# A hybrid GLA/SGU/PEER block on one core: other group sizes in the front, separate gather queues, and work moved between VectorE and GpSimd

## The chip, the core and the metric

The kernel runs on one core of a Trainium2 chip. The metric is the device time in microseconds (us) of one execution. A core has TensorE (PE; weight loads are listed as PEld), VectorE (DVE), ScalarE (ACT), GpSimd (POOL) and SyncE (SP), each with its own instruction stream, and 16 DMA engines that they share. SP starts most of the plain transfers; POOL starts the gathers, which fetch 128 rows by a list of indices.

## The reference, cut to what matters

```python
h = x + merged(GLA branch, SGU branch) @ w_out          # 1024 tokens, width 1024
n2 = rmsnorm(h, norm2_g)
# peer(n2):
q = (n2 @ w_q).reshape(T, 8, 2, 128)                    # 8 heads, two halves
s1, s2 = q[:, :, 0] @ sub_k1.T, q[:, :, 1] @ sub_k2.T   # 128 scores each
v1, i1 = top_k(s1, 16); v2, i2 = top_k(s2, 16)
cand = v1[..., :, None] + v2[..., None, :]              # 16 x 16 a head
vals, ci = top_k(cand, 16)
idx = i1[ci // 16] * 128 + i2[ci % 16]                  # 128 experts a token
gates = softmax(vals)
hid = einsum('tkd,td->tk', expert_u[idx], n2)           # 16384 experts in all
out = einsum('tk,tkd->td', gelu(hid) * gates, expert_v[idx])
y = rmsnorm(h + out, final_g)
```

All arrays are float32.

## The kernel before

The 1024 tokens are eight blocks of 128. The program has four stages.

**Front** (`front_all`): projections, both branches, the merge, the queries and their scores, for a group of blocks at a time. `GROUPS` gives the groups and, by a letter, each block's kind. Each group reads every weight block again: `load_w` loads 512 KB (`wraw`), ScalarE rounds it to a high half (`whi`, L242), GpSimd subtracts that from it (`wlo`, L243), and three matmuls per chunk (high by high, high by low, low by high) make one product of float32 quality (`mm3`; the tiles `pt` and `pn`).

**Top-k** (`topk_steps`, L583 to L654) runs on VectorE: per head the sixteen largest of both score halves, the sums of the candidates (`cd`, L605, four rectangles a head), the sixteen largest sums, then the decoding into expert numbers and gates. It is a queue of small steps, and so is the gathering; after each group of matmuls `pump(us)` gives every `Queue` a credit of `us` times its rate and runs steps for it. What of the queues is not done by the end is run by `drain()`.

**Blocks of kind g** fetch their experts. `u_steps`: 128 gathers of u rows (`gu`, POOL L741), and for each a dot with the block's row on VectorE (L735). `v_steps`: 128 gathers of v rows (`gv`, L822), four to a step, which 32-column matmuls (L809) sum into `gacc` in PSUM; after the last, VectorE adds `gacc` to the residual (`gres`, L834). The block that `ROWV` names is summed by rows instead: gather (L785), then a multiply-add on VectorE (`racc`, L781). In `all_v` the blocks go one after the other. A gather waits for a free buffer and, through `paced`, for the last matmul put out ahead of it.

**Blocks of kind d** compute all 16384 experts. `gate_steps` builds their gate matrix from one-hot rows: `gJ` on VectorE (L686), `gW` half on GpSimd (L692, with the gate already multiplied in) and half on ScalarE (a Square and a Relu, L695 and L696); products `gp` (L674) go to `g_d` in DRAM. `h_phase(i)` makes the hidden values of 128 experts for the four d blocks: 24 matmuls of 512 columns (`hp`, L914 to L916). `v_phase` multiplies four such sets of gated values with four blocks of v: 96 matmuls (`vp`, L973 to L975) into 8 PSUM tiles, each added to `dacc` on VectorE (L978). `split` rounds u and v blocks to halves: the high one on ScalarE (L900), the low one (`ul`, `vl`) on VectorE (L901). There are 128 `h_phase`s and 32 `v_phase`s. The first `HEAD` = 80 `h_phase`s run before the first `v_phase` and store their values (`a_d`); this is the *head*. The rest are mixed among the `v_phase`s, the *body*, by the list `order`. The *drain* is what follows the last `v_phase`.

```python
GROUPS = ("ggdd", "ggdd")
HEAD = 80
ROWV = (2,)
```

Tile buffers: three for `gu`, six for `gv`, two for `wraw`, three that u and v blocks share (`raw`), four each for `vh` and `vl`.

Of the kernel before, what the change touches and what calls it, by code (L numbers as in the profile page):

```python
# [33 lines left out]
GROUPS = ("ggdd", "ggdd")  # L34
HEAD = 80
# [4 lines left out]
GUB = 3  # L40
WZB = 2
ARB = 2
UAHEAD = 2
VAHEAD = 3
ROWV = (2,)
WRB = 2
TGB = 4
GAHEAD = 3
GPOOL = 2
RATE_TOPK = 0.55  # L50
RATE_TOPK2 = 1.0
RATE_UF = 0.75
RATE_UH = 1.0
RATE_GATHER = 0.9
# [12 lines left out]
def block_kernel(ctx: ExitStack, tc: tile.TileContext, a, out):  # L67
# [43 lines left out]
    S = {"state": state0}  # L111
# [115 lines left out]
    def front_all(groups, pump, after_group):  # L227
# [6 lines left out]
        def load_w(src, c0, n):  # L234
# [90 lines left out]
        def sgu_block(G, b):  # L325
# [23 lines left out]
        def decay_block(G, b):  # L349
# [5 lines left out]
            z = G["scr"][:, 4 + b, :]  # L355
# [52 lines left out]
        def branches(G):  # L408
# [20 lines left out]
            G["scr"] = fp.tile([P, 8, 512], F32, name="scr", tag="nBl")  # L429
# [135 lines left out]
        for n, G in enumerate(Gs):  # L565
            branches(G)
# [16 lines left out]
    def topk_steps(b, G):  # L583
# [7 lines left out]
        rc = tk.tile([P, HEADS], F32, name="rc")  # L591
        for h in range(HEADS):
# [5 lines left out]
            v = tk.tile([P, 2, TOPK], F32, name="v")  # L598
            for half in range(2):
                top16(v[:, half, :], ix[:, half, hs], s[:, half, :])  # L600
            cd = tk.tile([P, NCAND], F32, name="cd")
            o = 0
            for a0, na, nbb in RECTS:
                sh = [P, na, nbb]
                nc.vector.tensor_tensor(  # L605
                    cd[:, o:o + na * nbb].rearrange("p (i j) -> p i j", i=na),
                    v[:, 0, a0:a0 + na].unsqueeze(2).to_broadcast(sh),
                    v[:, 1, 0:nbb].unsqueeze(1).to_broadcast(sh), op=ALU.add)
                o += na * nbb
            yield 3.9  # L610
            top16(vals[:, hs], pos[:, hs], cd)
            yield 1.4
# [45 lines left out]
    def gate_steps(gb, b):  # L658
# [23 lines left out]
        for q in range(P // 4):  # L682
# [30 lines left out]
    ws, iTs, iis, wz, hvs = {}, {}, {}, [], {}  # L713

    def start_v(gv):
        pools["gatv"] = gv
        for r in range(WZB):
            wz.append(gv.tile([P, 4, 64], F32, name=f"wz{r}"))
            nc.vector.memset(wz[r], 0.0)
        pools["fg"] = bcast_row(gv, a["gf"], D, "fg")  # L720

    def gather_steps():
# [48 lines left out]
        def v_rows(b):  # L771
# [11 lines left out]
            for k in range(HK):  # L783
                v = pools["gatv"].tile([P, D], F32, name="gv", bufs=GVB)
# [8 lines left out]
            finish(gat, b, acc, pools["fg"], pools["gatv"].tile([P, D], F32, name="gv", bufs=GVB))  # L793
            yield 0

        def v_steps(b):
# [38 lines left out]
            finish(gat, b, res, pools["fg"], flat)  # L835
# [42 lines left out]
    def pump(us):  # L878
        for q in queues:
# [7 lines left out]
    def dense(pump):  # L887
        TP = TB // 2 if TB > 512 else TB
        NP = TB // TP
        with tc.tile_pool(name="dn", bufs=1) as dn, ExitStack() as dvx:  # L890
# [3 lines left out]
            def split(pool, dst, src):  # L894
# [50 lines left out]
            def gates(i):  # L945
                key, at = i < HEAD, i // G2
                if held.get(key, (None, None))[0] != at:
                    G = dv.tile([P, NB, P // GT, G2, GT], F32, name="G", bufs=4)
# [3 lines left out]
                    held[key] = at, G  # L952
                return held[key][1][:, :, :, i % G2, :]
# [27 lines left out]

            order, fresh = [], list(range(HEAD, P))
            for i in range(HEAD):
                k = (i + 1) * len(fresh) // HEAD - i * len(fresh) // HEAD
                order += [i] + fresh[len(order) - i:len(order) - i + k]
            prev, cur = None, []
            for n, i in enumerate(order):
# [10 lines left out]
                if len(cur) == GI or n == P - 1:  # L998
# [77 lines left out]
```

## Time and profile before

| | us |
|---|---|
| runs | 3521.14, 3527.49, 3520.89; median 3521.14 |
| the profiled execution | 3520.11 |
| its span (first to last instruction) | 3518.3 |
| PE busy | 3062.6 (87%) |
| DVE busy | 2272.3 (65%) |
| POOL busy | 1818.8 (52%) |
| ACT busy | 1028.0 (29%) |

| moment in the span | us |
|---|---|
| first dot with a gathered u row | 632.0 |
| first matmul of an `h_phase` | 1188.0 |
| first matmul of a `v_phase` | 1955.7 |
| last matmul of a `v_phase` | 3213.2 |

Busy times are sums of an engine's instructions over the whole span, so they hide what binds a stage; the moments above cut the span into the four stages. Matmuls are pipelined: their records overlap, and the distance between two starts, not the length of one, is what a matmul costs. The column PEclk of the windows view is the granted TensorE clock as a share of its full 2.4 GHz.

### The profile page before, as it was taken

Reading aid. Unit: us, or ns where it says so; the run is one execution under the profiler, and the core shown is the slowest. Engines: PE = TensorE matmul, PEld = TensorE weight load, DVE = VectorE, ACT = ScalarE, POOL = GpSimd, SP = SyncE. Lnnn points to the kernel's source line nnn. Section 1 sums busy time; section 2 is a strip of 40 time slices with the busy share of each in tenths; the row PEclk is TensorE's granted clock in tenths of the full one; section 3 lists DMA queues with packets and bytes.
Section 4 is the critical chain, followed back from the end, with each engine's and each line's share of the span. In section 5 each row is a group of like instructions: output and inputs, shape, how many; then the busy total and the mean of one; then the engine's idle time right before and its main releaser. Section 6 shows DMA issues by size and latency. Waiting matters only on the chain.

```text
span 3518.3 us, 41416 instructions
## 1 busy us (share of the span) xinstructions
PE 3062.6 (87%) x14244; PEld 2217.4 (63%) x14244; DVE 2272.3 (65%) x4978; ACT 1028.0 (29%) x1898; POOL 1818.8 (52%) x1433
## 2 busy tenths in 40 slices
PE   7999998878768589999999889999999798886665
PEld 6978987766656367666666666656667676674110
DVE  4262457999978768567533676555558999996000
ACT  3332333122122356526553222222222222221000
POOL 3334332556556588838784445444443566644443
PEclk9999998989879799999999999999999999997676
DMA  3223442566677878788779988899889999997776
GB/s 126 78 91 115 148 127 76 181 214 205 221 259 245 281 273 308 284 318 286 288 269 332 347 297 328 320 340 324 318 312 310 319 370 376 373 344 239 239 241 207
DMA packets 336548, 908.72 MB, mean 258 GB/s; under 512 B 33857, under 2 KB 124225, under 8 KB 335314
## 3 DMA queue, kind: packets, MB, share of 16 engines
q0 software_dynamic: 147456, 536.94, 43.5%
q1 hardware_dynamic: 188882, 369.14, 30.4%
q8 instruction: 112, 1.84, 0.2%
q14 instruction: 98, 0.80, 0.1%
HBM read 830.45 MB, written 75.50 MB: 257 GB/s over the span
## 4 chain that ended last, share of the span: by engine, by line
PE 46%; DVE 21%; DMA 14%; issue 11%; POOL 5%; ACT 1%; POOLq 0%; DVEq 0%; SPq 0%; ACTq 0%
PE gacc L809 8%; DMA gu<-in_pu,ii 7%; DVE gu L735 6%; DMA gv<-in_pv,iT 5%; PE hp L914 4%; PE hp L916 4%; PE hp L915 4%; POOL gu L741 3%; PE vp L973 3%; PE vp L974 3%; PE vp L975 3%; DVE racc L781 3%; PE gp L674 2%; PE pt L248 2%; PE pt L249 2%
## 5 line engine op out<-in xcount | busy, mean ns | idle before, releaser
L741 POOL DMA_INDIRECT gu<-in_pu,ii x512 | 595.9, 1164 | 565.5 <-DVE gu L735 324.2
L735 DVE SCALAR_TENSOR_TENSOR gu<-gu,gn 128x1024 f32<-128x1024 f32 x512 | 672.8, 1322 | 180.0 <-DMA gu<-in_pu,ii 167.6
L822 POOL DMA_INDIRECT gv<-in_pv,iT x384 | 414.8, 1080 | 553.7 <-PE gacc L809 463.9
L243 POOL TENSOR_TENSOR wlo<-wraw,whi 128x1024 fp32r<-128x1024 f32 x144 | 351.8, 2461 | 424.0 <-ACT whi L242 423.4
L809 PE MATMUL gacc<-gv,wz 128*32 128x512 f32 x1536 | 452.5, 724 | 108.3 <-DMA gv<-in_pv,iT 106.9
L914 PE MATMUL hp<-dnh,uh 128*128 128x512 f32 x1024 | 414.9, 405 | 54.1 <-ACT uh L900 52.8
L973 PE MATMUL vp<-vh,ah 128*128 128x512 f32 x1024 | 407.4, 407 | 42.2 <-DVE dacc L978 26.1
L974 PE MATMUL vp<-vl,ah 128*128 128x512 f32 x1024 | 413.4, 404 | 7.6 <-DVE vl L901 7.6
L916 PE MATMUL hp<-dnh,ul 128*128 128x512 f32 x1024 | 410.2, 401 | 7.5 <-DVE ul L901 7.0
L915 PE MATMUL hp<-dnl,uh 128*128 128x512 f32 x1024 | 409.7, 400 | 2.0 <-DVE dnl L178 2.0
L975 PE MATMUL vp<-vh,al 128*128 128x512 f32 x1024 | 396.0, 402 | 6.5 <-DVE al L962 6.5
L809 PEld LDWEIGHTS gacc<-gv,wz 128*32 128x32 f32 x1536 | 75.5, 119 | 357.9 <-DMA gv<-in_pv,iT 212.6
L692 POOL TENSOR_SCALAR gW<-iota_r,gT 128x128 f32<-128x128 bf16 x256 | 276.5, 1087 | 23.5 <-PE gp L674 11.8
L914 PEld LDWEIGHTS hp<-dnh,uh 128*128 128x128 f32 x1024 | 195.4, 191 | 129.7 <-ACT uh L900 65.5
L973 PEld LDWEIGHTS vp<-vh,ah 128*128 128x128 f32 x1024 | 199.3, 195 | 116.6 <-DVE dacc L978 43.7
L978 DVE TENSOR_TENSOR dacc<-dacc,vp 128x512 f32<-128x512 f32 x256 | 168.2, 683 | 122.7 <-PE vp L975 114.3
L974 PEld LDWEIGHTS vp<-vl,ah 128*128 128x128 f32 x1024 | 199.2, 195 | 67.4 <-issue 16.8
L916 PEld LDWEIGHTS hp<-dnh,ul 128*128 128x128 f32 x1024 | 194.4, 190 | 74.1 <-issue 21.8
L975 PEld LDWEIGHTS vp<-vh,al 128*128 128x128 f32 x1024 | 198.3, 194 | 67.6 <-issue 15.9
L901 DVE TENSOR_TENSOR ul<-raw,uh 128x1024 fp32r<-128x1024 f32 x128 | 157.3, 1229 | 125.0 <-ACT uh L900 96.5
L785 POOL DMA_INDIRECT gv<-in_pv,ii x128 | 178.7, 1396 | 114.3 <-DVE racc L781 45.6
L915 PEld LDWEIGHTS hp<-dnl,uh 128*128 128x128 f32 x1024 | 195.8, 191 | 56.6 <-issue 16.8
(271 smaller groups left out, 5737.6 us busy)
## 6 DMA issues: line engine op xcount, KB each, us to landing
raw<-in_ut SPq DMA_DIRECT2D x128, 512.0 KB
raw<-in_pv SPq DMA_DIRECT2D x128, 512.0 KB
wraw<-in_wt SPq DMA_DIRECT2D x80, 512.0 KB
g_d<-gst SPq DMA_DIRECT2D x8, 4096.0 KB
G<-g_d SPq DMA_DIRECT2D x256, 128.0 KB
a_d<-A SPq DMA_DIRECT2D x80, 256.0 KB
Ar<-a_d SPq DMA_DIRECT2D x80, 256.0 KB
wraw<-in_wq SPq DMA_DIRECT2D x32, 512.0 KB
```

Of the source, the lines that this page charges most:

```text
L243: nc.gpsimd.tensor_tensor(lo[:, :, sl], raw, hi[:, :, sl].bitcast(F32), op=ALU.subtract)
L692: nc.gpsimd.tensor_scalar(W[:, x, :], iota_r, i_, g_, op0=ALU.is_equal, op1=ALU.mult)
L735: queued(nc.vector.scalar_tensor_tensor(u, u, 1.0, n2, op0=ALU.mult, op1=ALU.mult, accum_out=hv[:, k:k + 1]), "dve")
L741: paced(nc.gpsimd.indirect_dma_start(out=u, out_offset=None, in_=a["pu"], in_offset=bass.IndirectOffsetOnAxis(ap=ii[:, k:k + 1], axis=0)))
L809: queued(nc.tensor.matmul(acc[32 * g:32 * g + 32, dh, :], z[:, g, 31 - r:63 - r], vs[g][:, dh * 512:(dh + 1) * 512], start=r == 0, stop=r ...
L822: paced(nc.gpsimd.indirect_dma_start(out=v, out_offset=None, in_=a["pv"], in_offset=bass.IndirectOffsetOnAxis(ap=iTs[b][:, t:t + 1], axis=0)))
L914: nc.tensor.matmul(ps[:, :TP], uh[:, cs], nh[:, c, ts_], start=c == 0, stop=False)
L915: nc.tensor.matmul(ps[:, :TP], uh[:, cs], nl[:, c, ts_], start=False, stop=False)
L916: mm = nc.tensor.matmul(ps[:, :TP], ul[:, cs], nh[:, c, ts_], start=False, stop=c == DC - 1)
L973: nc.tensor.matmul(ps, ah[:, bl], vh[:, ds_], start=x == 0, stop=False)
L974: nc.tensor.matmul(ps, ah[:, bl], vl[:, ds_], start=False, stop=False)
L975: mm = nc.tensor.matmul(ps, al[:, bl], vh[:, ds_], start=False, stop=x == n - 1)
```

## The change

- `GROUPS` becomes three groups of 2, 3 and 3 blocks. Blocks 0 to 3 are still of kind g and 4 to 7 of kind d. `HEAD` is 72. Each weight block is read three times instead of twice; in group 0 `wlo` is made on VectorE.
- The gathers' one queue, which took u and v steps in turns, becomes two with rates of their own; a u dot stands four gathers behind its gather instead of two; there are five `gu` buffers. The last g block (3) is the one summed by rows, not block 2.
- The candidate sums of all eight heads are made together: four operations a block instead of 32.
- `gW` is made on VectorE like `gJ`, for four tokens in one operation, and ScalarE multiplies the gates in. GpSimd and the Square/Relu pair have no part in it any more.
- `vl` is made on GpSimd instead of VectorE; u and v blocks have staging buffers of their own (three `rawu`, two `rawv`).
- The gate tiles `G` are held for one pair of indices; `order` sorts pairs of `h_phase`s; `fg` is loaded for each block that ends; some scratch tiles shrink with the group. `GVX` is 0, so its extra tiles are never taken.

```diff
-GROUPS = ("ggdd", "ggdd")
-HEAD = 80
+GROUPS = ("gg", "ggd", "ddd")
+HEAD = 72
-GUB = 3
+RAWB = {"u": 3, "v": 2}
+GUB = 5
-UAHEAD = 2
+UAHEAD = 4
-ROWV = (2,)
-WRB = 2
-TGB = 4
-GAHEAD = 3
+ROWV = (3,)
+WRB = 3
+TGB = 5
+GAHEAD = 2
-RATE_UF = 0.75
-RATE_UH = 1.0
-RATE_GATHER = 0.9
+RATE_U = (0.4, 0.9, 0.8)
+RATE_V = (0.2, 0.5, 0.5)
+RATE_VE = 1.2
...
-                nc.gpsimd.tensor_tensor(lo[:, :, sl], raw, hi[:, :, sl].bitcast(F32), op=ALU.subtract)
+                eng = nc.gpsimd if S["group"] else nc.vector
+                eng.tensor_tensor(lo[:, :, sl], raw, hi[:, :, sl].bitcast(F32), op=ALU.subtract)
...
+        o = 0
+        for a0, na, nbb in RECTS:
+            sh = [P, HEADS, na, nbb]
+            nc.vector.tensor_tensor(
+                cd[:, :, o:o + na * nbb].rearrange("p h (i j) -> p h i j", i=na),
+                v[:, :, 0, a0:a0 + na].unsqueeze(3).to_broadcast(sh),
+                v[:, :, 1, 0:nbb].unsqueeze(2).to_broadcast(sh), op=ALU.add)
+            o += na * nbb
...
+            queued(nc.vector.tensor_tensor(W, T[:, 0, qs].unsqueeze(2).to_broadcast([P, 4, P]),
+                                           iota_r.unsqueeze(1).to_broadcast([P, 4, P]), op=ALU.is_equal), "dve")
             for x in range(4):
                 t = 4 * q + x
-                i_, g_ = T[:, 0, t:t + 1], T[:, 2, t:t + 1]
-                if x < GPOOL:
-                    nc.gpsimd.tensor_scalar(W[:, x, :], iota_r, i_, g_, op0=ALU.is_equal, op1=ALU.mult)
-                else:
-
-                    queued(nc.scalar.activation(W[:, x, :], iota_r, AF.Square, scale=-1.0, bias=i_), "act")
-                    nc.scalar.activation(W[:, x, :], W[:, x, :], AF.Relu, scale=T[:, 3, t:t + 1], bias=g_)
+                queued(nc.scalar.activation(W[:, x, :], W[:, x, :], AF.Copy, scale=T[:, 2, t:t + 1]), "act")
...
     def pump(us):
+        if not q_u.its:
+            q_v.rate = RATE_VE
         for q in queues:
             q.run(us)
...
-                raw = dn.tile([P, D], F32, name="raw", bufs=3)
+                raw = pool.tile([P, D], F32, name="raw" + dst, bufs=RAWB[dst])
                 nc.sync.dma_start(raw, src)
                 nc.scalar.activation(hi, raw, AF.Copy)
-                last["dve"] = nc.vector.tensor_tensor(lo, raw, hi.bitcast(F32), op=ALU.subtract).ins
+                if dst == "u":
+                    last["dve"] = nc.vector.tensor_tensor(lo, raw, hi.bitcast(F32), op=ALU.subtract).ins
+                else:
+                    nc.gpsimd.tensor_tensor(lo, raw, hi.bitcast(F32), op=ALU.subtract)
...
+            pairs = sorted(range(P // G2), key=lambda n: (n + 0.5) / HEAD if n * G2 < HEAD
+                           else (n - HEAD // G2 + 0.5) / (P - HEAD))
+            order = [n * G2 + x for n in pairs for x in range(G2)]
...
-    q_topk, q_gat = Queue(RATE_TOPK), Queue(RATE_UF, turns=True)
+    q_topk, q_u, q_v = Queue(RATE_TOPK), Queue(RATE_U[0]), Queue(RATE_V[0])
...
-    q_gat.its.extend(gather_steps())
+    for q, it in zip((q_u, q_v), gather_steps()):
+        q.its.append(it)
```

What this does to the order of instructions is seen on GpSimd. In the front before, from its first weight block on:

```order
L243 TENSOR_TENSOR wlo<-wraw,whi 128x8x128 x88
L741 DMA gu<-in_pu,ii 128x1024 x4
L243 TENSOR_TENSOR wlo<-wraw,whi 128x8x128 x2
L741 DMA gu<-in_pu,ii 128x1024 x3
L243 TENSOR_TENSOR wlo<-wraw,whi 128x8x128
```

And after (L246 and L751 are the same two lines of code):

```order
L246 TENSOR_TENSOR wlo<-wraw,whi 128x8x128 x18
L751 DMA gu<-in_pu,ii 128x1024 x3
L246 TENSOR_TENSOR wlo<-wraw,whi 128x8x128 x2
L751 DMA gu<-in_pu,ii 128x1024 x2
L246 TENSOR_TENSOR wlo<-wraw,whi 128x8x128 x2
```

Of the 216 subtractions 76 are VectorE's (the 72 of group 0 and four of group 1 that are loaded during group 0's merge) and 140 GpSimd's, and the gathers begin after 18 instead of 88 of those that are left. In the body, GpSimd's row before had gathers alone:

```order
L741 DMA gu<-in_pu,ii 128x1024 x3
L822 DMA gv<-in_pv,iT 128x1024 x4
L741 DMA gu<-in_pu,ii 128x1024 x3
L822 DMA gv<-in_pv,iT 128x1024 x4
L741 DMA gu<-in_pu,ii 128x1024 x3
```

After, `vl` (L916) stands between them, two at a time, with nine gathers from pair to pair:

```order
L832 DMA gv<-in_pv,iT 128x1024 x4
L916 TENSOR_TENSOR vl<-rawv,vh 128x1024 x2
L751 DMA gu<-in_pu,ii 128x1024 x5
L832 DMA gv<-in_pv,iT 128x1024 x4
L916 TENSOR_TENSOR vl<-rawv,vh 128x1024 x2
L751 DMA gu<-in_pu,ii 128x1024 x5
```

GpSimd's end before, with the second half of block 3's four-row gathers (L822) after all others:

```order
L785 DMA gv<-in_pv,ii 128x1024
L741 DMA gu<-in_pu,ii 128x1024 x2
L822 DMA gv<-in_pv,iT 128x1024 x6
L741 DMA gu<-in_pu,ii 128x1024 x32
L822 DMA gv<-in_pv,iT 128x1024 x122
```

And after (L832 is the four-row gather, L795 the gather by rows):

```order
L916 TENSOR_TENSOR vl<-rawv,vh 128x1024 x2
L832 DMA gv<-in_pv,iT 128x1024 x4
L916 TENSOR_TENSOR vl<-rawv,vh 128x1024 x2
L832 DMA gv<-in_pv,iT 128x1024 x18
L795 DMA gv<-in_pv,ii 128x1024 x128
```

The last 128 gathers are now those of the block summed by rows, each of them followed by an add on VectorE, and 18 four-row gathers stand between the last `vl` and them. On TensorE 30 `gacc` matmuls follow the last `vp` where 256 did; 234 stand ahead of the first `vp` (256 before), and 504 among the `v_phase`s (256 before). The first `vp` comes after 74 `h_phase`s (81 before).

## Rows read from the trace of the kernel before

**Rows 1.** The page, its first part: busy time, share of the span, instructions.

```profile
PE 3062.6 (87%) x14244; PEld 2217.4 (63%) x14244; DVE 2272.3 (65%) x4978; ACT 1028.0 (29%) x1898; POOL 1818.8 (52%) x1433
```

**Rows 2.** Windows: stretch, length, busy us of PE, PEld, DVE, ACT, POOL; PEclk, DMA, GB/s.

```profile
0.00:470.00 470.00, 446.41 (x2648) 387.14 (x2649) 188.18 (x473) 166.21 (x296) 168.84 (x78) 0.99 0.35 112
470.00:1188.00 718.00, 557.15 (x2875) 467.69 (x2874) 628.88 (x1847) 178.96 (x297) 359.87 (x230) 0.86 0.63 201
590.00:1188.00 598.00, 446.83 (x2334) 376.64 (x2334) 541.52 (x1525) 134.24 (x237) 322.39 (x214) 0.85 0.68 220
1188.00:1955.00 767.00, 724.51 (x3463) 504.75 (x3462) 465.76 (x1248) 386.82 (x859) 547.89 (x491) 0.97 0.81 296
1955.00:2610.00 655.00, 622.32 (x2563) 405.13 (x2563) 411.51 (x606) 142.44 (x211) 295.93 (x259) 0.98 0.90 321
2610.00:3215.00 605.00, 530.59 (x2188) 421.08 (x2186) 557.64 (x750) 144.18 (x197) 327.82 (x252) 0.95 0.95 338
3215.00:3518.00 303.00, 181.60 (x513) 31.66 (x513) 20.30 (x59) 9.43 (x40) 118.50 (x126) 0.71 0.69 230
```

**Rows 3.** Timeline of the drain, POOL and DVE: start, length, instruction, [idle before it].

```profile
3298.69 0.94 POOL L822 DMA_INDIRECT gv<-in_pv,iT  x1 [3.97 <-PE gacc L809]
3299.93 0.94 POOL L822 DMA_INDIRECT gv<-in_pv,iT  x1 [0.30 <-issue]
...
3307.30 0.94 POOL L822 DMA_INDIRECT gv<-in_pv,iT  x1 [3.95 <-PE gacc L809]
...
3508.58 1.22 DVE L834 TENSOR_TENSOR gres<-gres,gacc 128x1024 f32<-128x1024 f32 x1 [273.54 <-PE gacc L809]
```

**Rows 4.** Groups: count | busy us, mean ns of one | idle before, releaser.

```profile
L735 DVE SCALAR_TENSOR_TENSOR gu<-gu,gn 128x1024 f32<-128x1024 f32 x512 | 672.8, 1322 | 180.0 <-DMA gu<-in_pu,ii 167.6
L243 POOL TENSOR_TENSOR wlo<-wraw,whi 128x1024 fp32r<-128x1024 f32 x144 | 351.8, 2461 | 424.0 <-ACT whi L242 423.4
L901 DVE TENSOR_TENSOR vl<-raw,vh 128x1024 fp32r<-128x1024 f32 x128 | 154.9, 1221 | 14.8 <-ACT vh L900 14.7
L605 DVE TENSOR_TENSOR cd<-v 128x16 f32<-128x16 f32 (+2 forms) x256 | 92.7, 380 | 0.0
L686 DVE TENSOR_TENSOR gJ<-gT,iota_r 128x512 f32<-128x512 f32 x128 | 88.6, 704 | 106.2 <-PE gp L674 87.3 <-issue 15.3 <-ACT gT L665 3.2
L781 DVE SCALAR_TENSOR_TENSOR racc<-gv,w,racc 128x1024 f32<-128x1024 f32 x128 | 164.2, 1283 | 0.4
```

**Rows 5.** Tiles: shortest/median/longest in ns, first and last start, forms.

```profile
L735 DVE SCALAR_TENSOR_TENSOR gu<-gu,gn x512: 1168/1220/6408, 632.0 to 3230.0; 128x1024 f32<-128x1024 f32 x171
L605 DVE TENSOR_TENSOR cd<-v x256: 109/164/5007, 456.5 to 1699.6; 128x24 f32<-128x24 f32 x64, 128x8 f32<-128x8 f32 x64
```

**Rows 6.** Timeline of the front, DVE and POOL.

```profile
805.90 6.41 DVE L735 SCALAR_TENSOR_TENSOR gu<-gu,gn 128x1024 f32<-128x1024 f32 x1
...
806.47 4.74 POOL L243 TENSOR_TENSOR wlo<-wraw,whi 128x1024 fp32r<-128x1024 f32 x2
```

**Rows 7.** Windows with the tile `wlo` alone: PE, PEld, POOL.

```profile
470.00:1188.00 718.00, 282.64 (x783) 154.80 (x782) 184.09 (x76) 0.86 0.63 201
```

**Rows 8.** Timeline of the body, PE.

```profile
2100.68 0.40 PE L975 MATMUL vp<-vh,al 128*128 128x512 f32 x1
2100.91 0.39 PE L973 MATMUL vp<-vh,ah 128*128 128x512 f32 x1
```

**Rows 9.** Windows of the body's first half: `vp`, `hp`, `gacc` alone, PE first.

```profile
1955.00:2610.00 655.00, 367.38 (x1475) 277.33 (x1476) 78.54 (x120) 0.98 0.90 321
1955.00:2610.00 655.00, 146.66 (x576) 106.59 (x575) 14.93 (x26) 0.98 0.90 321
1955.00:2610.00 655.00, 128.87 (x512) 21.52 (x512) 1.21 (x1) 1.43 (x4) 0.98 0.90 321
```

**Rows 10.** Windows: 100 us of the body, columns as in rows 2.

```profile
2900.00:3000.00 100.00, 88.47 (x356) 69.75 (x355) 98.74 (x120) 22.87 (x29) 64.69 (x48) 0.93 1.00 368
```

**Rows 11.** Waits: who waited for whom, us in all, times, longest us.

```profile
POOL gv L822 <- PE gacc L809: 463.9, 82, 20.9
```

More of the change, by code (lines that the diff above doesn't have):

```diff
@@ L110, in block_kernel @@
     nc.vector.memset(state0, 0.0)
-    S = {"state": state0}
+    S = {"state": state0, "group": 0}
     last = {}
@@ L297, in norm1_load @@
             G["kv"] = []
-            xq = fp.tile([P, 2, D], F32, name="xq", tag="q")
+            xq = fp.tile([P, 1, D], F32, name="xq", tag="q")
             for b in range(G["nb"]):
-                x = xq[:, b, :] if b < 2 else fp.tile([P, D], F32, name="xs", tag=f"s{2 * b - 4}")
+                x = xq[:, b, :] if b < 1 else fp.tile([P, D], F32, name="xs", tag=f"s{2 * b - 2}")
                 t0 = (G["g0"] + b) * P
@@ L333, in sgu_block @@
             r = rstd_of(wk, v, 1, "rv")
-            vn = G["scr"][:, 4 + b % 2, :]
+            vn = G["scr"][:, G["nb"] + b % 2, :]
             nc.vector.tensor_scalar(vn, sv, mv[:, 0:1], r, op0=ALU.subtract, op1=ALU.mult)
             ps = sm_ps("mix")
-            t = G["scr"][:, 6 + b % 2, :]
+            t = G["scr"][:, b % 2, :]
             for g in range(4):
@@ L354, in decay_block @@
             la = G["scr"][:, b, :]
-            z = G["scr"][:, 4 + b, :]
+            z = G["scr"][:, G["nb"] + b, :]
             nc.scalar.activation(z, zp, AF.Copy)
@@ L565, in front_all @@
         for n, G in enumerate(Gs):
+            S["group"] = n
             branches(G)
@@ L591, in topk_steps @@
         rc = tk.tile([P, HEADS], F32, name="rc")
+        v = tk.tile([P, HEADS, 2, TOPK], F32, name="v")
+        cd = tk.tile([P, HEADS, NCAND], F32, name="cd")
         for h in range(HEADS):
@@ L597, in topk_steps @@
             nc.sync.dma_start(s, s_d[b][:, 2 * h:2 * h + 2, :])
-            v = tk.tile([P, 2, TOPK], F32, name="v")
             for half in range(2):
[L600 to L612, printed above, removed]
+                top16(v[:, h, half, :], ix[:, half, hs], s[:, half, :])
+            yield 2.8
+        o = 0
[6 more added lines that the diff above has]
+            o += na * nbb
+        yield 1.5
+        for h in range(HEADS):
+            hs = slice(h * TOPK, (h + 1) * TOPK)
+            top16(vals[:, hs], pos[:, hs], cd[:, h, :])
+            yield 1.2
         y, z = yz[:, 0, :], yz[:, 1, :]
@@ L718, in start_v, with gv_tile, final_g @@
             wz.append(gv.tile([P, 4, 64], F32, name=f"wz{r}"))
-            nc.vector.memset(wz[r], 0.0)
-        pools["fg"] = bcast_row(gv, a["gf"], D, "fg")
+            nc.gpsimd.memset(wz[r], 0.0)
+    def gv_tile():
+        turn[0] += 1
+        if "gvx" in pools and turn[0] % (GVB + GVX) < GVX:
+            return pools["gvx"].tile([P, D], F32, name="gvx", bufs=GVX)
+        return pools["gatv"].tile([P, D], F32, name="gv", bufs=GVB)
+    def final_g():
+        return bcast_row(pools["gatv"], a["gf"], D, "fg", "gv", GVB)
     def gather_steps():
@@ L792, in v_rows @@
                 add()
-            finish(gat, b, acc, pools["fg"], pools["gatv"].tile([P, D], F32, name="gv", bufs=GVB))
+            finish(gat, b, acc, final_g(), pools["gatv"].tile([P, D], F32, name="gv", bufs=GVB))
             yield 0
@@ L834, in v_steps @@
             nc.vector.tensor_tensor(res, res, flat, op=ALU.add)
-            finish(gat, b, res, pools["fg"], flat)
+            finish(gat, b, res, final_g(), flat)
             yield 0
@@ L936, in dense @@
             tkx.close()
-            q_gat.rate = RATE_GATHER
-            dv = dvx.enter_context(tc.tile_pool(name="dv", bufs=1))
+            q_u.rate, q_v.rate = RATE_U[2], RATE_V[2]
+            dv = pools["gvx"] = dvx.enter_context(tc.tile_pool(name="dv", bufs=1))
             acc = [dv.tile([P, D], F32, name=f"dacc{b}") for b in range(NB)]
@@ L945, in gates @@
             def gates(i):
-                key, at = i < HEAD, i // G2
-                if held.get(key, (None, None))[0] != at:
-                    G = dv.tile([P, NB, P // GT, G2, GT], F32, name="G", bufs=4)
+                at = i // G2
+                if held.get("at") != at:
+                    G = dv.tile([P, NB, P // GT, G2, GT], F32, name="G", bufs=3)
                     for s in range(NB):
@@ L951, in gates @@
                                           g_d[DB[s]][:, :, at * G2:(at + 1) * G2, :].rearrange("q j i t -> j q (i t)"))
-                    held[key] = at, G
-                return held[key][1][:, :, :, i % G2, :]
+                    held["at"], held["G"] = at, G
+                return held["G"][:, :, :, i % G2, :]
             def gated(i, A):
@@ L979, in v_phase @@
                     done(b)
[L982 to L985, printed above, removed]
+            pairs = sorted(range(P // G2), key=lambda n: (n + 0.5) / HEAD if n * G2 < HEAD
+                           else (n - HEAD // G2 + 0.5) / (P - HEAD))
+            order = [n * G2 + x for n in pairs for x in range(G2)]
             prev, cur = None, []
@@ L1013, in block_kernel @@
     fx0.close()
+    q_topk.rate, q_u.rate, q_v.rate = RATE_TOPK2, RATE_U[1], RATE_V[1]
     with tc.tile_pool(name="psm2", bufs=2, space=PSUM) as psm, \
```

17 lines of the change are left out of this document (8 added, 9 removed).

## The prediction

> **What bounds the kernel now.** I read the page's totals first [rows 1]: TensorE is busy 3063 of 3518 us and nothing else is near it. But that is an average over stages with different limits, so I cut the span with the windows view [rows 2]. The front is the first 1188 us: in its first 470 us TensorE is busy 95% and VectorE 40%, while from 590 to 1188 us VectorE is busy 541.5 of 598 us, TensorE 75%. There VectorE sets the pace. The head, to 1955 us, is TensorE's (94%). The body has two halves: to 2610 us TensorE is busy 95%; to 3215 us it falls to 88% while VectorE rises to 92%, because block 2's row adds stand there. In the last 303 us TensorE does 182 us of gather products, VectorE 20, and the DMA engines are 69% busy: nothing is full. The timeline shows why [rows 3]: POOL issues gathers 1.24 us apart, then waits about 4 us for `gacc`, so four gathers take 8.61 us, 2.15 us each, and the last result is added only at 3508.6.
>
> Against each other, 1188 + 767 + 1260 + 303 = 3518 us. The profiled execution took 3520.1, 1.8 more than its span and 1.0 below the median of the three runs; the sum is made against the profiled one and that 1 us is ignored.
>
> **Front: 1188 to 1101.** TensorE gets the same columns in smaller matmuls; only the weight blocks rise, 144 to 216, as three groups read them. Group 0 is now two blocks instead of four and TensorE-bound as the first 470 us were. Take its two eighths of the front's 1004 us of TensorE [rows 2], at 95%, and 6 us more since the first wait for data, part of the missing 5%, does not shrink: 270 us.
> The other two groups go by VectorE. Its front was 188 + 629 = 817 us. Added: 76 `wlo` of group 0 at the 1.22 us that the same subtraction `vl` takes on VectorE [rows 4], 93; one block's top-k more, since 198 rather than 164 of 272 index searches now come before the first `ul`. The head prices a block: 466 us less 117 dots at 1.314, 82 `ul` at 1.22 and 89 of `gJ` leave 123 for 3.2 blocks, so 38. Removed: eight dots, 10; candidate sums, 256 of 0.38 against 32 over eight heads [rows 4]. At the median of 0.164 the 256 cost 42 [rows 5]; with 8 us for the 32 (an estimate: 0.25 each, half as long again as that median for rows eight times as long) the whole gain lies between 42 - 8 = 34 and 93 - 8 = 85, three quarters of it in the front; I take 41.
> POOL's `wlo` holds VectorE up: a dot takes 1.22 us alone (the median, [rows 5]) but 6.41 beside two `wlo` [rows 6]. All 512 dots together lost 672.8 - 512 x 1.22 = 48 us to the 38 pairs after 470 us [rows 4, 7], 1.3 a pair. After, 140 `wlo` make 70 pairs, all in the VectorE-bound part: 32 more, 42 us. What the Trainium skill says, in "SBUF — State Buffer", section "Who interferes with whom", is that a VectorE instruction with two SBUF inputs contends with a GpSimd one that reads SBUF, and that the later one fully blocks until the earlier ends. The 6.41 us dot agrees. By the rule at its worst every pair would hold VectorE for its whole 4.92 us, the front would be 280 us longer and the sum 3730; the 48 us lost so far speak for far less.
> So 817 + 93 + 38 - 10 - 41 + 42 = 939 us, of which group 0 takes 94 + 93 = 187. The remaining 752, at the present share of 0.906, take 830; 270 + 830 is about 1101. Bounds: 1022 if TensorE's 1004 us and some 18 us of start alone bound it, 1188 and above if the pairs cost more. POOL's 140 x 2.46 and 137 gathers x 1.24 make 514 us and fit. The 72 added weight loads, 38 MB, fall where the DMA engines are 35 to 68% busy.
>
> **Head: 767 to 730.** HEAD 72 and the new order put 74 `hp` phases before the first `vp` instead of 81: seven phases of 24 matmuls at 0.227 us [rows 8], 38 us off. 22 fewer `gacc` at 0.50 us of TensorE (129 us for 256, [rows 9]), 11 off. POOL loses 256 one-hots, VectorE gets 128 of the `gJ` shape, 90 us [rows 4], and 39 more dots, 51, less 38 of top-k and the rest of the candidate sums: about 545 of 730 us, still below TensorE. I add 12 us for its bursts; the ends are 0 and 50, a tenth of its work. ScalarE keeps 512 small ops.
>
> **Body: 1260 to 1404.** It takes in what stood elsewhere: 3072 `vp` matmuls as before, but 54 phases instead of 47, and 504 `gacc` instead of 256. (3072 + 1296) x 0.227 = 991 us. In the first half of the old body 1475 + 576 such matmuls account for 466 us of 655; 189 are left for 256 program matmuls of `gacc` (512 records), 0.74 us each with their stalls [rows 9]. 504 of them: 373. Then the low half of v: 128 leave VectorE at 1.22 us and come to POOL at 2.46 (the price of `wlo`, same shape). POOL's order is the danger, since `vl` now stands behind gathers that wait for gather buffers. One duration's difference, 1.24 us, showing at each of 32 `v` phases is 40. Total 1404. Bounds: 1243 without stalls, and 1417 at the share of 0.877 of the second half with everything else equal. VectorE loses 155 us of `vl` and 164 of row adds here, so that even 64 pairs at 1.3 us find room.
>
> **Drain: 303 to 214.** Instead of 128 gathers in 4-row products there are 18 and then all 128 rows of block 3, each added by VectorE at 1.28 us [rows 4]. No quad waits stand between them: six buffers stream. The DMA engines moved 368 GB/s where they were full [rows 10], so 0.52 MB takes 1.42 us: 182 us, with 22 for the last quads and the lead and 10 for the finish. Bounds: 1.24 per gather by POOL's issue, so 191 in all; 2.15 as now, 307 in all.
>
> Larger buffers, `wz` on POOL, `fg` per block, the smaller scratch tiles and the unused v tiles cost nothing that TensorE does not cover; one `bcast_row` more at the end is within the 10.
>
> **Sum:** 1101 + 730 + 1404 + 214 + 1.8 = 3451, taken as **3450 us**, 2% less. Gain 87 + 37 + 89 against a loss of 144.
>
> **The rivals.**
> *Slower: `vl` late on POOL.* Between two `v` phases POOL's row reads two `vl`, nine gathers, two `vl`. Nine issues 11.2, one wait for `gacc` of 464 / 82 = 5.7 [rows 11], four `vl` 9.8, and 1 for ScalarE's `vh`: 27.7 us. The last `vl` buffers come free only as a phase ends; TensorE then has 42 `vp` matmuls that do not need them (9.5), a phase of `hp` (5.4) and eight `gacc` (2.5): 17.4. It would stand 10.3 us in the 25 gaps that hold one phase, 257 in place of the 40: **3667**. For it: POOL is in order and already waits 82 times. Against: the seven wider gaps, and gathers that are paced by the same TensorE. It turns the sign from about 4.4 us a gap.
> *Slower: the port.* VectorE always has an operation ready in the last two groups, so a pair meets one far more often: with 3.1 us a pair, midway between 1.3 and 4.92, 70 x 1.8 / 0.906 = 139 more: **3589**. By a row alone, the 6.41 us dot, it is real; how often is open. It turns the sign from 0.9 us a pair more.
> *TensorE-bound throughout.* The front at 1022, head 717, body 1305 (half of the stalls, no late `vl`), drain 214: **3260**. For it: 95% in every stage that VectorE leaves alone.
> *The change does not do what it says.* Row gathers do not stream but take the 2.15 us of now, 307 in the drain: **3543**; POOL's gathers then had a limit of their own and moving them gained nothing.
>
> **How the numbers follow.** Forecast 0.46, own range 3370 to 3510; late `vl` 0.18; port 0.12; TensorE-bound 0.17; rows that do not stream 0.07. The range leaves out the late `vl` and reaches to the others: 3250 to 3610. A measurement here tells 0.2%, 7 us, from no change. Faster: 0.45 + 0.17 = 0.62. Same: 0.01 of the forecast and 0.04 of the rows that do not stream, whose drain may lie under that. Slower: 0.18 + 0.12 + 0.03 = 0.33.
>
> **What would show it.** First `hp` near 1101 us and VectorE over 90% busy before it; if `wlo` pairs hold dots beyond 3 us on the mean, the port rival. First `vp` near 1831. In the body the idle time before `vp` of `vl`: about 40 us in all by the forecast, 250 by its rival. After the last `vp` some 210 us, with `gv` 1.4 us apart and no wait for `gacc` between rows. The prediction is wrong if the front stays above 1188, if the body passes 1480, or if the last stage stays near 300.

## The result, and the profile after

The change makes the kernel slower: 3613.5 us (3607.9 to 3615.0, four runs) against 3521.0 us beside it, a ratio of 1.0257, 95% interval 1.0239 to 1.0274. The forecast was 3450 us, the other way, and its range ended at 3610.

The busy line of the page stands against [rows 1]: no engine's total changes by much.

```profile
PE 3090.6 (86%) x15420; PEld 2332.3 (65%) x15420; DVE 2410.7 (67%) x4862; ACT 1087.0 (30%) x2036; POOL 1888.7 (52%) x1303
```

The windows view by stages answers to [rows 2] (the front in two parts, group 0 and the rest; the body in two parts; columns as there).

```profile
0.00:280.00 280.00, 264.87 (x2112) 255.95 (x2113) 178.32 (x422) 141.24 (x244) 4.53 (x11) 0.99 0.59 191
280.00:1177.00 897.00, 756.03 (x4586) 720.09 (x4586) 749.20 (x2041) 284.00 (x491) 516.44 (x281) 0.89 0.61 196
1177.00:1904.00 727.00, 675.52 (x3285) 478.97 (x3284) 535.44 (x1169) 358.13 (x841) 347.13 (x274) 0.97 0.88 331
1904.00:2890.00 986.00, 891.00 (x3508) 598.16 (x3509) 618.76 (x852) 200.49 (x289) 643.22 (x437) 0.95 0.85 295
2890.00:3378.00 488.00, 485.33 (x1875) 275.77 (x1874) 154.09 (x218) 99.21 (x160) 218.04 (x164) 1.00 0.65 221
3378.00:3612.00 234.00, 17.83 (x63) 3.37 (x61) 174.94 (x164) 3.92 (x12) 159.37 (x138) 0.55 0.90 325
```

| stage | before | forecast | after |
|---|---|---|---|
| front | 1188 | 1101 | 1177 |
| head | 767 | 730 | 727 |
| body | 1260 | 1404 | 1474 |
| drain | 303 | 214 | 234 |

So the loss is the body's: 214 us more, of which 144 were forecast, and the front gave back 11 us where 87 were forecast. The body's two windows differ. While u gathers run, to 2890 us, TensorE is busy 90% and GpSimd 65%; after the last dot (2886.5) TensorE is busy 99% at the full granted clock.

The waits and the groups of the change (as in [rows 11] and [rows 4], over the whole span) name what is new in the first part.

```profile
POOL gv L832 <- PE gacc L819: 541.9, 89, 15.1
PE vp L989 <- POOL vl L916: 68.4, 22, 8.1
```

```profile
L745 DVE SCALAR_TENSOR_TENSOR gu<-gu,gn 128x1024 f32<-128x1024 f32 x512 | 747.9, 1481 | 118.1 <-DMA gu<-in_pu,ii 114.9
L989 PE MATMUL vp<-vl,ah 128*128 128x512 f32 x1024 | 422.9, 414 | 68.5 <-POOL vl L916 68.4
L916 POOL TENSOR_TENSOR vl<-rawv,vh 128x1024 fp32r<-128x1024 f32 x128 | 313.9, 2467 | 106.6 <-ACT vh L912 103.7
L977 DVE TENSOR_TENSOR al<-Ar,ah 128x512 fp32r<-128x512 f32 x72 | 67.8, 957 | 10.7 <-ACT ah L976 7.3 <-PE vp L990 2.6 <-PE vp L989 0.4
```

A `vl` takes 2.47 us on GpSimd, as forecast. TensorE stood idle 68 us for it. Beside that the dots have become longer, 1.48 us on the mean against 1.32, and `al` (the form shown) 0.957 against 0.688 before, though nothing was changed in either. One of the waits for `vl`, in the timeline of the body (the last idle time in brackets is TensorE's):

```profile
2366.79 0.94 POOL L832 DMA_INDIRECT gv<-in_pv,iT  x1 [4.26 <-PE gacc L819]
...
2371.87 0.94 POOL L751 DMA_INDIRECT gu<-in_pu,ii  x1 [0.30 <-issue]
...
2375.61 0.94 POOL L751 DMA_INDIRECT gu<-in_pu,ii  x1 [0.30 <-issue]
2376.56 4.67 POOL L916 TENSOR_TENSOR vl<-rawv,vh 128x1024 fp32r<-128x1024 f32 x2
2378.97 0.80 PE L989 MATMUL vp<-vl,ah 128*128 128x512 f32 x1 [8.08 <-POOL vl L916]
```

GpSimd waits 4.26 us for `gacc`, puts out four `gv` and four `gu`, and only then comes to the `vl`; TensorE waits 8.08 us. In the drain the rows do stream: the 128 row gathers were put out from 3399.5 to 3594.3 us, 1.53 us apart.

### The profile page after: what moved, and what is told of

The parts are those of the page before. It is cut to its first block, busy times and chain, and to the rows that moved or that the text cites. A ratio compares the mean times of both kernels' runs of the same rounds, so it can differ in the third digit from the quotient of the medians.

```text
span 3612.0 us, 43844 instructions
## 1 busy us (share of the span) xinstructions
PE 3090.6 (86%) x15420; PEld 2332.3 (65%) x15420; DVE 2410.7 (67%) x4862; ACT 1087.0 (30%) x2036; POOL 1888.7 (52%) x1303
## 4 chain that ended last, share of the span: by engine, by line
PE 32%; issue 8%; POOL 6%; DMA 6%; DVE 4%; ACT 0%; SPq 0%; POOLq 0%; DVEq 0%; ACTq 0%
PE gacc L819 8%; PE vp L989 5%; PE vp L990 5%; PE vp L988 5%; PE hp L929 3%; PE hp L930 3%; PE hp L931 3%; POOL gu L751 2%; POOL gv L795 2%; POOL vl L916 2%; DMA gv<-in_pv,iT 1%; DVE gu L745 1%; DMA gu<-in_pu,ii 1%; PE gp L680 1%; DMA gv<-in_pv,ii 1%
## 5 line engine op out<-in xcount | busy, mean ns | idle before, releaser
L751 POOL DMA_INDIRECT gu<-in_pu,ii x512 | 631.3, 1233 | 476.3 <-DVE gu L745 149.0
L745 DVE SCALAR_TENSOR_TENSOR gu<-gu,gn 128x1024 f32<-128x1024 f32 x512 | 747.9, 1481 | 118.1 <-DMA gu<-in_pu,ii 114.9
L832 POOL DMA_INDIRECT gv<-in_pv,iT x384 | 442.4, 1152 | 645.8 <-PE gacc L819 541.9
L246 POOL TENSOR_TENSOR wlo<-wraw,whi 128x1024 fp32r<-128x1024 f32 x140 | 349.7, 2518 | 430.9 <-ACT whi L244 415.0
L989 PE MATMUL vp<-vl,ah 128*128 128x512 f32 x1024 | 422.9, 414 | 68.5 <-POOL vl L916 68.4
L990 PE MATMUL vp<-vh,al 128*128 128x512 f32 x1024 | 415.1, 408 | 2.0 <-DVE al L977 2.0
L916 POOL TENSOR_TENSOR vl<-rawv,vh 128x1024 fp32r<-128x1024 f32 x128 | 313.9, 2467 | 106.6 <-ACT vh L912 103.7
L914 DVE TENSOR_TENSOR ul<-rawu,uh 128x1024 fp32r<-128x1024 f32 x128 | 177.8, 1390 | 200.1 <-ACT uh L912 162.2
L244 ACT ACTIVATE whi<-wraw 128x1024 fp32r<-128x1024 f32 x216 | 220.8, 1053 | 244.8 <-PE pt L252 90.0
L912 ACT ACTIVATE uh<-rawu 128x1024 fp32r<-128x1024 f32 x128 | 135.2, 1057 | 285.6 <-PE hp L930 261.6
```

The lines of the kernel that those rows point to most:

```text
L246: eng.tensor_tensor(lo[:, :, sl], raw, hi[:, :, sl].bitcast(F32), op=ALU.subtract)
L745: queued(nc.vector.scalar_tensor_tensor(u, u, 1.0, n2, op0=ALU.mult, op1=ALU.mult, accum_out=hv[:, k:k + 1]), "dve")
L751: paced(nc.gpsimd.indirect_dma_start(out=u, out_offset=None, in_=a["pu"], in_offset=bass.IndirectOffsetOnAxis(ap=ii[:, k:k + 1], axis=0)))
L832: paced(nc.gpsimd.indirect_dma_start(out=v, out_offset=None, in_=a["pv"], in_offset=bass.IndirectOffsetOnAxis(ap=iTs[b][:, t:t + 1], axis=0)))
L916: nc.gpsimd.tensor_tensor(lo, raw, hi.bitcast(F32), op=ALU.subtract)
L989: nc.tensor.matmul(ps, ah[:, bl], vl[:, ds_], start=False, stop=False)
```

## The experiments

Each kernel ran beside the kernel before; the differences below are against those runs.

**e1_vl_dve: the change, with `vl` back on VectorE.**

```diff
-                if dst == "u":
-                    last["dve"] = nc.vector.tensor_tensor(lo, raw, hi.bitcast(F32), op=ALU.subtract).ins
-                else:
-                    nc.gpsimd.tensor_tensor(lo, raw, hi.bitcast(F32), op=ALU.subtract)
+                last["dve"] = nc.vector.tensor_tensor(lo, raw, hi.bitcast(F32), op=ALU.subtract).ins
```

> The change with the low half of v back on VectorE, nothing else. Theory A (late vl on GpSimd costs the body what the trace puts down to it, 80 us of TensorE's weight loads waiting for vl, and the port lock on VectorE a little more): the body falls from 1474 to about 1390 us, the total from 3613 to about 3530, and the wait for vl is below 20 us. Rival B (the vl waits are only where the body's excess shows; the excess is gather products and the lower granted clock, and VectorE gets 155 us more to do): the body stays within 15 us of 1474, the total between 3595 and 3630.

3477.7 us, 0.9891 of before (0.9862 to 0.9919). This one line is worth 135 us and turns the sign, 52 us more than theory A expected, which had priced the wait for `vl` as the trace puts it down. Front 1172, head 726, body 1359, drain 219. Its body, in the windows view, and the body of the change:

```profile
1898.00:3257.00 1359.00, 1342.72 (x5412) 853.62 (x5410) 805.13 (x1193) 299.94 (x451) 559.29 (x485) 1.00 0.84 296
```

```profile
1904.00:3378.00 1474.00, 1376.34 (x5381) 873.92 (x5382) 772.85 (x1069) 299.69 (x449) 861.25 (x601) 0.96 0.78 271
```

TensorE is now busy 99% of the body at the full clock: without `vl` on GpSimd the body is TensorE's own work. And VectorE got 124 `vl` (151 us) back in its body for only 805 - 773 = 32 us of busy time. Its other operations are shorter here, first of all the 226 dots of the body, in the change and then in e1:

```profile
L745 DVE SCALAR_TENSOR_TENSOR gu<-gu,gn 128x1024 f32<-128x1024 f32 x226 | 324.8, 1463 | 11.5 <-DMA gu<-in_pu,ii 11.5
L745 DVE SCALAR_TENSOR_TENSOR gu<-gu,gn 128x1024 f32<-128x1024 f32 x226 | 270.9, 1220 | 23.3 <-DMA gu<-in_pu,ii 23.3
```

Count times the difference of the means gives 55 us for the dots, 26 for `al`, 19 for `ul`, and 112 us for all groups of the body: that much of the 151 us had come back as longer operations. This lengthening of VectorE's operations beside GpSimd's work is called the hold below.

**e2_rows23: the change, with blocks 2 and 3 by rows** (`ROWV = (2, 3)`).

> The change with blocks 2 and 3 summed by rows instead of block 3 alone. Theory A (the body is bound by TensorE, and each gather product costs it 0.585 us): about 226 products fewer in the body, 132 us off, 164 us more on VectorE, which has 700 us free there; drain as it is, some 220 us; total 3470 to 3490. Rival C (the body is bound by what feeds it, gathers and vl on GpSimd's queue): the body loses under 40 us and the total stays above 3570.

3507.5 us, 0.9965 (0.9949 to 0.9981). The body fell by 97 us to 1377, less than the 132 expected, with 452 of 1012 `gacc` records gone: TensorE's own work counts in the body, and its waits took a part of it back (the idle time for `vl` rose from 68 to 82 us, that for `dacc` from 13 to 34). The total is 17 us above theory A's range too.

**h2_b_groups3_dve: the kernel before, with three groups and group 0's `wlo` on VectorE.**

```diff
-GROUPS = ("ggdd", "ggdd")
+GROUPS = ("gg", "ggd", "ddd")
...
-                nc.gpsimd.tensor_tensor(lo[:, :, sl], raw, hi[:, :, sl].bitcast(F32), op=ALU.subtract)
+                eng = nc.gpsimd if S["group"] else nc.vector
+                eng.tensor_tensor(lo[:, :, sl], raw, hi[:, :, sl].bitcast(F32), op=ALU.subtract)
```

> The kernel before with groups of 2, 3 and 3 and with group 0's low weight halves on VectorE; queues, candidate sums, top-k, head, body and drain as before. Theory A (the front gains little from groups alone, because a chain of small VectorE steps runs three times instead of twice and waits behind dots): front 1170 to 1195 us, total 3500 to 3530. Rival D (groups alone would give the 70 to 90 us that were forecast, and the deeper gather queue or the candidate sums took them back): front 1090 to 1130, total about 3440.

3555.4 us, 1.0112 (1.0049 to 1.0174), and a front of 1291 us: neither theory. Indices were ready earlier, and at the old rate 219 dots instead of 152 came to stand in the front. So this run did not hold the dots fixed; e4 and f3 do, at none.

**e4_no_u_front: the change, with no u gathers in the front** (`RATE_U = (0.0, 0.9, 0.8)`), and **f3_b_no_u_front: the same for the kernel before** (`RATE_UF = 0.0`).

> The change with no u gathers and so no dots in the front (they follow in the head and the body, so the end gets later: only the front is read). VectorE's front loses 136 dots at 1.22, 166 us, and the port lock on them, about 75. If VectorE's load sets the front's pace: the front falls from 1177 to about 1000 to 1040, near TensorE's own work. If the chains of small steps between the groups set it, whatever VectorE does beside them: the front stays above 1130.

> The kernel before with no u gathers in the front (only the front is read; the end gets later). The change without them had a front of 1085 us. If three groups instead of two gain time in the front by themselves: here 1120 us or more. If groups gain nothing and the 11 us come from fewer dots and cheaper candidate sums: here 1085 or less.

The fronts are 1085 us with three groups and 1074 with two (single runs, 3716.7 and 3767.1 us in all, their ends late as expected). The windows of what follows the first group in each, e4 and then f3:

```profile
280.00:1085.00 805.00, 732.53 (x4591) 699.87 (x4591) 507.92 (x1764) 280.56 (x490) 340.20 (x141) 0.94 0.40 127
```

```profile
470.00:1074.00 604.00, 541.43 (x2866) 456.33 (x2865) 421.13 (x1567) 175.65 (x292) 182.24 (x75) 0.92 0.33 105
```

VectorE is busy 63% and 70% there, TensorE 91% and 90%, and still the fronts end at 1085 and 1074. e4's front lies between the two that were expected (1000 to 1040, above 1130). Three groups, with the other changes of the front, are no shorter than two. 140 dots with their gathers then cost the change 1177 - 1085 = 92 us, 0.66 each; 152 cost the kernel before 1188 - 1074 = 114, 0.75 each. Of the 1.22 us that a dot takes alone, about half is hidden.

**f4_b_vl_pool: the kernel before, with `vl` on GpSimd.** The edit is that of the change in `split`; the staging ring stays one.

> The kernel before with the low half of v on GpSimd, nothing else (its staging ring of three buffers stays shared by u and v). If vl is late wherever it stands behind gathers on GpSimd: body from 1260 to 1340 or more, total 3600 or more. If what makes it late is the change's own order and its two staging buffers: body within 40 us of 1260.

3662.8 us, 1.0379 (1.0336 to 1.0422): 136 us above its runs of before (the next expectation says 141, against another set of them), as much as in the change. The body rose by 93 us, the drain by 47. So it needs neither the change's order nor its two staging buffers. The bodies of f4 and of the kernel before:

```profile
1963.00:3314.00 1351.00, 1190.84 (x4747) 841.81 (x4746) 985.69 (x1185) 285.30 (x405) 904.07 (x615) 0.94 0.86 299
```

```profile
1955.00:3215.00 1260.00, 1152.91 (x4749) 826.21 (x4748) 969.15 (x1355) 286.62 (x408) 623.74 (x510) 0.97 0.92 330
```

VectorE's busy time rose by 16 us though 126 `vl` (154 us) and 21 dots, which now follow the last `vp`, had left the body: by the groups, its other operations are 178 us longer, dots 74, `racc` 34, `Ar` 24, `al` 21. TensorE's idle time for `vl` is only 28 us.

**d1_b_vl_twice: the kernel before, with `vl` on VectorE and a second subtraction on GpSimd that nobody waits for.**

```diff
-                nc.scalar.activation(hi, raw, AF.Copy)
+                cp = nc.scalar.activation(hi, raw, AF.Copy)
                 last["dve"] = nc.vector.tensor_tensor(lo, raw, hi.bitcast(F32), op=ALU.subtract).ins
+                if dst == "v":
+                    if "vx" not in pools:
+                        pools["vx"] = pool.tile([P, D], F32, name="vx")
+                        nc.gpsimd.memset(pools["vx"], 0.0)
+                    ex = nc.gpsimd.tensor_tensor(pools["vx"], pools["vx"], pools["vx"], op=ALU.subtract)
+                    tc.add_manual_dep(ex.ins, cp.ins.name, SYNC, reason="pace")
```

> The kernel before, with vl where it was on VectorE, and beside it a subtraction of the same size on GpSimd for each v block, on a scratch tile that nobody reads, released by the same ScalarE copy (vh). GpSimd has the same work and the same lock on VectorE as with vl on it, but TensorE waits for none of it. If the 141 us of vl on GpSimd are TensorE's waiting for a vl that stands behind gathers: total within 30 us of the kernel before. If they are the lock on VectorE and the time that GpSimd loses for issuing gathers: 100 us or more above it.

3657.4 us, 1.0370 (1.0341 to 1.0399): 131 us, with nobody waiting. The theory that the price is TensorE's wait for a late `vl` falls for the kernel before. Its groups on VectorE:

```profile
L901 DVE TENSOR_TENSOR vl<-raw,vh 128x1024 fp32r<-128x1024 f32 x128 | 241.1, 1895 | 10.3 <-ACT vh L900 9.9 <-issue 0.3
L984 DVE TENSOR_TENSOR dacc<-dacc,vp 128x512 f32<-128x512 f32 x256 | 167.6, 681 | 119.3 <-PE vp L981 104.4 <-issue 14.8
L968 DVE TENSOR_TENSOR al<-Ar,ah 128x512 fp32r<-128x512 f32 x80 | 66.6, 837 | 2.5 <-issue 1.1 <-ACT ah L967 0.9 <-PE vp L981 0.4
```

`vl`, with both inputs in SBUF, takes 1.90 us on the mean instead of 1.22 [rows 4]; `dacc`, which reads one input from PSUM, stays at 0.68.

**d4_b_vl_pool_vbufs5: f4 with five buffers for `vh` and `vl`** (`n = 2 if dst == "u" else GI + 1`).

> The kernel before with vl on GpSimd and five buffers for each of vh and vl instead of four, so that one vl of the next group of four can be made a whole phase earlier. If lateness against TensorE is the price, one block of lead takes a fair part of it: total 30 to 90 us below the 3663 of four buffers. If the order of the gathers on GpSimd sets it whatever the lead: within 20 us of 3663.

3684.9 us, 1.0448 (1.0419 to 1.0477), slower than with four; neither theory said so. The body went back to 1260 us, but the drain rose to 461: 56 dots and 33 row adds came to stand after the last `vp`, against 28 and none. The lead and the moved gathers are not told apart by it.

**g4_b_memset, g1_vl_dve_gub4, g2_gub4_sub, g3_gub4_memset.** g4 is d1 with two fills in place of the subtraction, which write SBUF and read none. g1 is e1 with four u buffers and dots three gathers behind, which makes room for the scratch tile; g2 adds d1's subtraction to it, g3 the fills.

```diff
+                    for n in range(2):
+                        ex = nc.gpsimd.memset(pools["vx"], 0.0)
+                        tc.add_manual_dep(ex.ins, cp.ins.name, SYNC, reason="pace")
```

> The kernel before with two fills of a scratch tile on GpSimd for each v block (0.97 us each, 1.94 in all, against 2.05 for the undisturbed subtraction of the run d1_b_vl_twice), released by the same copy. They write SBUF and read none. If the lock on VectorE was the price of that run (VectorE's operations there were 162 us longer in the body): total within 40 us of the kernel before. If GpSimd's time, lost for the gathers, was the price: 90 us or more above it.

> The change with vl on VectorE and four u buffers with dots three behind, instead of five and four: the base for the next two runs. The order leaves 118 gather products after the last v phase instead of 30, so some 30 to 60 us above 3478.

> The run g1_vl_dve_gub4 with the subtraction on a scratch tile on GpSimd beside it, as in d1_b_vl_twice. If TensorE's wait for a late vl was the price in the change's body (TensorE stood idle 68 us for it), this run, where nobody waits, is within 40 us of g1_vl_dve_gub4. If the lock or GpSimd's time was: 80 us or more above it.

> The run g1_vl_dve_gub4 with two fills of a scratch tile on GpSimd for each v block. By the lock: within 15 us of g1_vl_dve_gub4, whatever g2_gub4_sub gives. By GpSimd's time: as far above it as g2_gub4_sub.

| | time, us | ratio to before | added by the GpSimd work |
|---|---|---|---|
| before + subtraction (d1) | 3657.4 | 1.0370 (1.0341 to 1.0399) | 131 |
| before + fills (g4) | 3558.1 | 1.0111 (1.0081 to 1.0140) | 38 |
| change, `vl` on VectorE, four u buffers (g1) | 3491.1 | 0.9923 (0.9893 to 0.9953) | |
| g1 + subtraction (g2) | 3558.3 | 1.0111 (1.0082 to 1.0141) | 67 |
| g1 + fills (g3) | 3500.2 | 0.9948 (0.9928 to 0.9968) | 9 |

In g4, `vl` on VectorE is back at its old length:

```profile
L901 DVE TENSOR_TENSOR vl<-raw,vh 128x1024 fp32r<-128x1024 f32 x128 | 155.0, 1221 | 15.0 <-ACT vh L900 15.0
```

The fills keep GpSimd nearly as long (body: 856 us busy in g4, 903 in d1) and hold VectorE up by nothing. The body took 1366 us in d1 and 1274 in g4, against 1260 before. So of the subtraction's 131 us in the kernel before, some 93 are the hold on VectorE and 38 GpSimd's time, if the two simply add. Added to g1, the same split is 58 and 9 us (the 9 are inside the intervals); g2's 67 us lie between the two that were expected (within 40, 80 or more), and g1 itself is 13 us above e1, where 30 to 60 were expected.

For the `vl` that the change really uses, the two parts can be seen but not divided. From e1 to the change the body grew by 115 us: TensorE's idle time by 81 (98 against 16), 64 of them for `vl` (68.4 against 4.7) and 12 for `dacc`, and its matmul time by 34 (1376 against 1343), at a granted clock of 0.96 against 1.00. So there the late `vl` is the larger part of what TensorE shows; in the kernel before, where TensorE waits 28 us for `vl` and d1 is as slow with no reader, it is the hold. How far the hold itself makes a `vl` late is not shown, and g2's 67 us cannot be taken from the 135, since g2 has `vl` on VectorE, where it is itself held up by 75 us.

The Trainium skill's rule, in "SBUF — State Buffer", section "Who interferes with whom", is borne out in the three parts that were tried: an operation with two SBUF inputs is held while GpSimd reads (1.90 us against 1.22), one with a single SBUF input is not (0.68), and a GpSimd operation that only writes holds VectorE up by nothing (1.221 us).

**d2_vl_dve_rows2: e1 with block 2 by rows and block 3 by products, as before** (`ROWV = (2,)`).

> The change with vl on VectorE and block 2 summed by rows, block 3 by gather products as before. The forecast's step on the swap (gather products into the body, row adds into the drain) was a small loss: here the body should lose some 230 products, 100 to 135 us of its 1359, and the drain should grow from 219 to about 300; total 3410 to 3460. If the swap was a gain by itself: total above 3478.

3444.7 us, a ratio of 0.9767: each against its own runs of before, 82 us less where e1 is 42 us less, so 40 us below e1. Body 1222 (137 less), drain 320 (101 more). The swap of the blocks alone is a loss: the products make the drain 101 us longer than row adds do, but a body in which TensorE has no room 137 us.

**f1_vl_dve_rows23, f2_b_rows23, t4_front_u: two blocks by rows.** f1 is e1 with `ROWV = (2, 3)`, f2 is the kernel before with `ROWV = (2, 3)`, and t4 is f1 with other rates:

```diff
-RATE_U = (0.4, 0.9, 0.8)
-RATE_V = (0.2, 0.5, 0.5)
-RATE_VE = 1.2
+RATE_U = (0.75, 1.0, 0.8)
+RATE_V = (0.2, 0.7, 0.7)
+RATE_VE = 1.4
```

> The change with the low half of v on VectorE and blocks 2 and 3 both summed by rows. If the two losses of the body are separate (late vl 115 to 130 us, 230 gather products at 0.43 to 0.58 us each), they add: body about 1265 us, total 3370 to 3400, below both kernels. If row adds and vl together make VectorE the body's bound: body above 1320, total above 3440.

> The kernel before with blocks 2 and 3 summed by rows: its drain has 128 row gathers and adds instead of 256 gather products. If a row gather costs what the change's drain shows (about 1.52 us against 2.15): drain 303 to about 220, body as it was, total about 3435 to 3450. If the drain's pace is the gathers' own landing time whatever follows them: drain within 20 us of 303, total above 3495.

> The change with vl on VectorE, blocks 2 and 3 by rows, and higher rates for the gathers (u 0.75 in the front instead of 0.4; v 0.7 instead of 0.5). A dot in the front has cost 0.66 to 0.75 us there; a row gather left for the drain costs 1.5. Some 85 dots more in the front, 60 us; some 90 row gathers fewer in the drain, 130 us: total about 3300. If the front's price rises with its load (the kernel before with three groups and 219 dots had 1291 us): 3350 or more.

| | us | ratio | front, head, body, drain |
|---|---|---|---|
| f2 | 3433.1 | 0.9728 (0.9690 to 0.9766) | 1182, 766, 1264, 217 |
| f1 | 3363.4 | 0.9525 (0.9495 to 0.9555) | 1178, 728, 1225, 234 |
| t4 | 3331.9 | 0.9442 (0.9419 to 0.9465) | 1281, 738, 1221, 93 |

One number in the kernel before (f2) is worth 94 us, nearly all of it in the drain: 217 instead of 303. In f1 both losses of the change are undone and add: 135 us by e1, some 105 by e2, some 250 together. t4 trades 122 more dots in the front, 103 us (0.84 each, more than the 0.66 of the first 140), for 92 fewer row adds in the drain, 141 us; it is the fastest version here, 5.6% below the kernel before, though 32 us above what was expected.

## Why the prediction was wrong, step by step

- **`vl` on GpSimd was mis-sized, and this turned the sign.** The forecast's 40 us ("one duration's difference, 1.24 us, showing at each of 32 `v` phases") measured 135, 115 of them in the body. Without this term the change would have been 1.1% faster (e1). Two things stand in its place. The late `vl` was there as the slower rival described it, but at 68 us of idle time, not 257, with TensorE at a lower clock beside it. The other is the hold on VectorE, which the forecast had weighed in the front and then passed over in the body, in the sentence that "even 64 pairs at 1.3 us find room". The 124 `vl` of the body, 62 pairs, lengthened VectorE's other operations by 112 us in the change, 1.8 a pair; in the kernel before 126 did so by 178. Room on VectorE's average did not help: in d1 it is busy 83% of the body, and 131 us were lost. How the 135 us divide between the two is not shown.
- **The prediction's own signs did not catch this.** The idle time for `vl`, 68 us, came out nearer to its 40 than to its rival's 250, and none of its three signs of being wrong was reached (front 1177, body 1474, drain 234).
- **The front was mis-sized by 76 us, in the step "the remaining 752, at the present share of 0.906, take 830".** The work was right: VectorE was busy 749 us after group 0, and group 0 took 280 us (270 forecast). (That VectorE's work was met so closely is in part luck: the price of a block's top-k was worked out with 117 dots in the head, where the trace has 104; it is 47 us rather than 38.) The share was wrong: 749 of 897 is 0.835. The step took VectorE's 91% before for the cause of the front's length. With no dots at all, and VectorE at 63%, that part still took 805 us. The front stands on something else, and dots lengthen it by 0.66 to 0.84 us each. What sets the 1074 to 1085 us, where TensorE is 90% busy after group 0, was not taken apart: the rival's 1022 us, TensorE alone, is missed by 52 to 63; that it is the chain of small steps of each group is only argued.
- **Two other terms of the body were off and cancelled, by luck.** The change's body has 1012 `gacc` records; from one start to the next they cost 0.30 us each, 300 us in all, where the forecast took 0.37 a record and 373. `vp` and `hp`, forecast at 0.227 us each and 991 in all, took 1064 in e1, from start to start, though the granted clock was 1.00 there. So e1's body, 1359 us, is what the forecast had without its `vl` term, 1364, and the body's miss of 70 us is the `vl` term's 75, less these 5.
- **The head** was right to 3 us (727 against 730).
- **The drain** was right in kind: rows stream, TensorE is out of it. A gather took 1.53 us, not 1.42; 234 against 214 us. The swap of blocks was priced as a loss and measured as one (40 us, d2).
- **The port rival** had the right mechanism in the wrong stage: in the front the pairs cost the dots no more than was forecast (the 140 dots there took 1.77 us on the mean, 76 us above 1.22 in all, 1.1 for each of the 70 pairs against 1.3).

## What to carry to other kernels

Moving an operation from VectorE to GpSimd relieves VectorE only by what the hold on its two-input operations leaves (here some 150 us left the body, and its other operations there became 112 us longer in the change and 178 in the kernel before), and this has to be priced in every stage in which the two run side by side. An engine that is 91% busy need not be what a stage waits for: take its load away once, with the rest as it is, before building a sum on its share. Put work where its engine is idle: one block's products cost 101 us more than row adds in the drain, but 137 us in a body that is TensorE's, while the row adds find room on VectorE in that body (f1).

## What was not expected of the hardware

- The hold is as strong as it is: 128 subtractions of 2.05 us (the median in d1) on GpSimd cost the whole kernel 131 us with no reader, and fills of about the same length 38.
- GpSimd itself was hardly slowed in the change (2.47 us for `vl` on the mean against 2.40 for the median), while VectorE's operations in the body became 112 us longer.
